# The transfers around a triangular substitution, moved from ScalarE's queue to GpSimd's

## Chip, cores and metric

The kernel runs on one core of a Trainium2 chip. The metric is the time of one execution on the device in microseconds (us). The kernel before was timed in three runs. All times below that have a place in the span are counted from the start of the span of one profiled execution.

## What is computed

One layer of a hybrid encoder on 256 tokens of width 2048: a gated linear attention (GLA) and a gated delta net run side by side on the normalised input, are merged by gates, and are followed by an MLP, a small input embedding and a last norm. The change lies in the delta net. For each head and each chunk of 64 tokens it needs the inverse of a lower triangular matrix:

```python
k_beta = k * beta[..., None]
a = jnp.where(strict, jnp.einsum('bhncd,bhnsd->bhncs', k_beta, k) * decay, 0.0)
t_mat = lax.linalg.triangular_solve(eye + a, jnp.broadcast_to(eye, a.shape), left_side=True,
                                    lower=True, unit_diagonal=True)
u = jnp.einsum('bhncs,bhnsv->bhncv', t_mat, v * beta[..., None])
w = jnp.einsum('bhncs,bhnsd->bhncd', t_mat, k_beta * jnp.exp(gcum)[..., None])
```

## The kernel before

All weights are streamed from HBM in fp32 and multiplied in two parts. The generator `weights` loads 1 MB into `raw` on SyncE's queue, ScalarE rounds it to `whi` (L101), VectorE subtracts to get the rest `wlo` (L102), and TensorE multiplies both parts: L114 to L116 in `stream`, L131 and L135 in `stream_t`. `whi` and `wlo` have three buffers each, so that ScalarE and VectorE may run ahead of TensorE by that much and no more.

The mixers are computed in a loop over four passes (`for h in range(GH)`, L353). A pass makes one GLA head and four delta net heads of two token blocks each, so eight matrices of 128x128. In the order of the program a pass computes k and q of the delta net, the small vectors, and then `af`, the triangular matrices (L459, VectorE). L461 on GpSimd masks their companion `at`.

The inverse is built from diagonal blocks of 32x32. There are 32 of them in a pass, and they are laid out one to a partition so that VectorE can run the substitution on all of them at once:

- `af` goes to DRAM tensor `da` in four DMAs (L468), and comes back as `a32`, 32 partitions of 1024 values (L470). `a32` takes the tile `cacc`, which has one buffer and also serves the short convolution.
- GpSimd has set `t32` to the identity (L472, L473). Then 31 steps of two VectorE instructions each follow, L479 and L481, the first of which waits for `a32`. They lie among the weight splits L102 in VectorE's queue.
- L483 copies the result, transposed within each block, into `u32`, which lies over `a32` in `cacc`. `t32` is stored to `dt` (L484) and `u32` to `du` (L485).
- From there four DMAs fill the diagonal blocks of `u_bd` (L489), two those of `t11` (L491) and one `tb` (L492). Each of them has to wait until `dt` or `du` has landed. TensorE reads them first in L574 to L576, where the off-diagonal blocks are made.

After that the program takes v of the delta net. Its short convolution writes `cacc` anew: four instructions of ScalarE (L378), one per head, and twelve of VectorE (L381), each group after its L378. The first L378 has to wait until `u32` has been read out of `cacc` by the DMA of L485. The weights of the GLA's streams go on at the same time.

All these DMAs are issued by ScalarE (`SC.dma_start`). An engine works through its own queue in order, and a DMA that waits holds up what is queued behind it on the engine that issues it.

Which instruction comes when on each engine isn't written out by hand: the program is given to a planner (`tile.TileContext(nc, schedule_with_timeline_sim=True)`, L864), which plays it through with a model of each instruction and fixes the order on every engine from it. Among instructions that are ready at the same time the one that comes earlier in the program goes first.

Of the kernel before, what the change touches and what calls it, by code (L numbers as in the profile page):

```python
# [37 lines left out]
def hybrid_block(ctx: ExitStack, tc: tile.TileContext, A: dict, out: bass.AP):  # L38
    nc = tc.nc
    V, SC, GP, TE, SY = nc.vector, nc.scalar, nc.gpsimd, nc.tensor, nc.sync  # L40
# [34 lines left out]
    def T4(tag, bufs=None, dt=F32):  # L75
        return mp.tile([P, 4, S], dt, tag=tag, bufs=bufs, name=tag)
# [222 lines left out]
    u_bd = mp.tile([P, 8, P], F32, name="u_bd")  # L299
    t11 = mp.tile([64, 8, 64], F32, name="t11")  # L300
# [52 lines left out]
    for h in range(GH):  # L353
# [58 lines left out]
        for i, src in enumerate((kT, qT)):  # L412
            for t in range(NT):
# [4 lines left out]
                for hd in range(4):  # L418
                    c = i * 8 + t * 4 + hd
# [22 lines left out]
        af = T4("af").rearrange("p a (b c) -> p (a b) c", b=2)  # L442
# [22 lines left out]
        da, dt_, du = (dram.tile([32, 32, 32], F32, name=n) for n in ("da", "dt", "du"))  # L465
        for b in range(4):
            bs = slice(b * 32, (b + 1) * 32)
            SC.dma_start(da[b * 8:(b + 1) * 8].rearrange("i s c -> s i c"), af[bs, :, bs])  # L468
        a32 = T4("cacc")[0:32].rearrange("p a b -> p (a b)").rearrange("p (s c) -> p s c", s=32)
        SC.dma_start(a32, da)  # L470
        t32 = mp.tile([P, NT, 512], F32, tag="og", name="t32").rearrange("p a b -> p (a b)")[0:32]
        GP.memset(t32, 0.0)  # L472
        GP.memset(t32[:, 0:1024:33], 1.0)  # L473
        t32 = t32.rearrange("p (c s) -> p c s", c=32)
# [6 lines left out]
            V.tensor_tensor(t32[:, j + 1:, 0:m], t32[:, j + 1:, 0:m], tv, ALU.subtract)  # L481
        u32 = a32
        V.tensor_copy(u32, t32.rearrange("p c s -> p s c"))  # L483
        SC.dma_start(dt_, t32)  # L484
        SC.dma_start(du, u32)  # L485
        tb = mp.tile([P, 8, 32], F32, tag="tmp", name="tb")
        for b in range(4):
            bs, ds = slice(b * 32, (b + 1) * 32), slice(b * 8, (b + 1) * 8)
            SC.dma_start(u_bd[bs, :, bs], du[ds].rearrange("i s c -> s i c"))  # L489
            if b < 2:  # L490
                SC.dma_start(t11[bs, :, bs], dt_[ds].rearrange("i c s -> c i s"))  # L491
        SC.dma_start(tb[64:96], dt_[16:24].rearrange("i c s -> c i s"))  # L492

        vT = qkv("v", O_DV, 32)
        rv = mp.tile([P, NT, 4, P], F32, name="rv")
# [185 lines left out]
        for kp in range(2):  # L681
            pz = mx3(2, S)
            for kk in range(2):
                for t in range(NT):
                    c = (kp * 2 + kk) * P
# [182 lines left out]
```

## Time and profile before

| | |
|---|---|
| Time, median of 3 runs | 1858.05 us (1855.92 to 1859.32) |
| Time of the profiled execution | 1857.95 us |
| Span of the profiled execution | 1856.2 us |
| TensorE matmuls (PE) busy | 1827.8 us, 98% of the span |
| VectorE (DVE) busy | 1180.2 us, 64% |
| ScalarE (ACT) busy | 946.6 us, 51% |
| GpSimd (POOL) busy | 77.5 us, 4% |
| Mean granted clock of TensorE | 0.996 |
| Bytes moved by DMA | 334.02 MB, 180 GB/s in the mean |

The busy time of an engine doesn't contain the issuing of DMAs on it; those stand in the timeline as ACTq, SPq, or as DMA_DIRECT2D on POOL. The busy time of a matmul is modelled and longer than its step, since matmuls overlap. In the rows a bracket at the end of a line holds the time for which the engine stood before the instruction, and what ended that.

### The profile page before, as it was taken

What the parts mean: (1) busy time and instruction counts of PE and PEld (TensorE: products, weight loads), DVE (VectorE), ACT (ScalarE), POOL (GpSimd) and SP (SyncE); (2) the same over time, 40 slices, a digit from 0 to 9 for tenths busy, and PEclk for the clock granted to TensorE, in tenths of its full rate; (3) what the DMA queues carried; (4) which work ended last, traced back from release to release, by engine and by line L of the source; (5) the groups of instructions that cost most, each with busy time, mean ns of one, the idle gap of its engine ahead of it and who ended that gap; (6) DMA issues with size and microseconds to landing.
All of it is one profiled execution on the core that took longest, in us unless ns stands there. A gap on an engine that the chain in (4) does not pass through costs nothing.

```text
span 1856.2 us, 24598 instructions
## 1 busy us (share of the span) xinstructions
PE 1827.8 (98%) x9796; PEld 1551.0 (84%) x9796; DVE 1180.2 (64%) x1637; ACT 946.6 (51%) x1324; POOL 77.5 (4%) x100
## 2 busy tenths in 40 slices
PE   8999999999999999999999999999999999999998
PEld 7887888878888788887888888888888888888887
DVE  5686577864768647686455655555556555565665
ACT  6745556455564655645545544444444434344654
POOL 3110011000110001100000000000000000000000
PEclk9999999999999999999999999999999999999999
DMA  7555446554455545565465665656656565655453
GB/s 239 148 185 169 159 149 192 168 172 160 155 179 187 178 150 159 159 205 167 144 233 191 184 192 182 198 187 188 196 183 194 191 190 193 187 188 195 162 201 137
DMA packets 245236, 334.02 MB, mean 180 GB/s; under 512 B 21680, under 2 KB 148992, under 8 KB 244736
## 3 DMA queue, kind: packets, MB, share of 16 engines
q1 hardware_dynamic: 231488, 325.47, 54.4%
q10 hardware_dynamic: 12992, 4.34, 1.0%
q0 software_dynamic: 640, 2.63, 0.4%
q8 instruction: 77, 1.26, 0.3%
q14 instruction: 39, 0.32, 0.0%
HBM read 328.74 MB, written 3.67 MB: 179 GB/s over the span
## 4 chain that ended last, share of the span: by engine, by line
PE 92%; DMA 3%; DVE 2%; ACT 2%; issue 1%; ACTq 1%; SPq 0%; POOLq 0%; POOL 0%; DVEq 0%
PE mm L131 24%; PE mm L115 16%; PE mm L116 16%; PE mm L114 16%; PE mm L135 13%; DMA du<-cacc 1%; DMA raw<-in_w_in 1%; PE mx L457 1%; DMA x_sb<-in_x 1%; DVE wlo L102 1%; ACT whi L101 1%; DVE cacc L381 1%; PE mx L562 0%; PE mx L168 0%; ACTq L489 0%
## 5 line engine op out<-in xcount | busy, mean ns | idle before, releaser
L102 DVE TENSOR_TENSOR wlo<-raw,whi 128x1024 fp32r<-128x1024 f32 x604 | 743.8, 1234 | 532.0 <-ACT whi L101 523.3
L101 ACT ACTIVATE whi<-raw 128x1024 fp32r<-128x1024 f32 x604 | 638.8, 1060 | 746.5 <-PE mm L116 389.3
L131 PE MATMUL mm<-act,whi 128*128 128x512 f32 x1984 | 542.7, 395 | 0.0
L131 PEld LDWEIGHTS mm<-act,whi 128*128 128x128 f32 x1984 | 339.7, 189 | 45.8
L115 PE MATMUL mm<-wlo,act 128*128 128x512 f32 x864 | 343.1, 397 | 8.9 <-DVE wlo L102 8.9
L114 PE MATMUL mm<-whi,act 128*128 128x512 f32 x864 | 339.2, 393 | 3.2 <-ACT whi L101 3.2
L135 PEld LDWEIGHTS mm<-act,wlo 128*128 128x128 f32 x1984 | 304.0, 189 | 43.0 <-issue 1.0
L116 PE MATMUL mm<-whi,act 128*128 128x512 f32 x864 | 338.9, 392 | 0.0
L135 PE MATMUL mm<-act,wlo 128*128 128x256 f32 x1984 | 317.4, 281 | 0.0
L115 PEld LDWEIGHTS mm<-wlo,act 128*128 128x128 f32 x864 | 163.1, 189 | 44.0 <-DVE wlo L102 10.4
L116 PE MATMUL mm<-whi,ul 128*128 128x512 f32 x512 | 199.6, 390 | 0.0
L114 PE MATMUL mm<-whi,uh 128*128 128x512 f32 x512 | 199.5, 390 | 0.0
L115 PE MATMUL mm<-wlo,uh 128*128 128x512 f32 x512 | 199.3, 389 | 0.0
L114 PEld LDWEIGHTS mm<-whi,act 128*128 128x128 f32 x864 | 162.8, 188 | 38.3 <-ACT whi L101 4.9
L116 PEld LDWEIGHTS mm<-whi,act 128*128 128x128 f32 x864 | 163.1, 189 | 33.7 <-issue 1.0
L116 PEld LDWEIGHTS mm<-whi,ul 128*128 128x128 f32 x512 | 96.1, 188 | 19.9
L115 PEld LDWEIGHTS mm<-wlo,uh 128*128 128x128 f32 x512 | 96.1, 188 | 19.8
L114 PEld LDWEIGHTS mm<-whi,uh 128*128 128x128 f32 x512 | 96.1, 188 | 19.6
L381 DVE SCALAR_TENSOR_TENSOR cacc<-zT,convw,cacc 128x255 f32<-128x255 f32 (+2 forms) x144 | 61.0, 477 | 18.0 <-ACT cacc L378 18.0
L757 DVE SCALAR_TENSOR_TENSOR x_sb<-mm,r2sq,x_sb 128x512 f32<-128x512 f32 x64 | 45.1, 746 | 12.2 <-PE mm L116 12.2
L479 DVE TENSOR_TENSOR tmp<-cacc,t 32x31 f32<-32x31 f32 (+15 forms) x124 | 40.6, 328 | 4.4 <-DMA cacc<-da 1.5
L481 DVE TENSOR_TENSOR t<-t,tmp 32x31 f32<-32x31 f32 (+15 forms) x124 | 40.8, 329 | 2.8
(311 smaller groups left out, 1230.6 us busy)
## 6 DMA issues: line engine op xcount, KB each, us to landing
raw<-in_w_in SPq DMA_DIRECT2D x143, 1024.0 KB, 4.9
raw<-in_w_up SPq DMA_DIRECT2D x64, 1024.0 KB, 5.6
raw<-in_w_down SPq DMA_DIRECT2D x64, 1024.0 KB, 4.9
raw<-in_w_out SPq DMA_DIRECT2D x16, 1024.0 KB, 4.9
raw<-in_w_ple_gate SPq DMA_DIRECT2D x16, 1024.0 KB, 4.9
x_sb<-in_x POOLq DMA_DIRECT2D x1, 2048.0 KB, 12.4
raw<-in_w_ple_proj SPq DMA_DIRECT2D x4, 512.0 KB, 3.8
out<-x_sb SPq DMA_DIRECT2D x8, 256.0 KB, 2.5
```

The source lines that it names most:

```text
L101: SC.activation(hi[:, :, :c], raw[:, kk:kk + g, :c], AF.Copy)
L102: V.tensor_tensor(lo[:, :, :c], raw[:, kk:kk + g, :c], hi[:, :, :c].bitcast(F32), ALU.subtract)
L114: TE.matmul(pt[:, t, :n], xh[:, k, ts], hi, start=(k == 0), stop=False)
L115: TE.matmul(pt[:, t, :n], xh[:, k, ts], lo, start=False, stop=False)
L116: TE.matmul(pt[:, t, :n], xl[:, k, ts], hi, start=False, stop=(k == nk - 1))
L131: TE.matmul(pt[c // 2][:, c % 2, :], hi[:, c * P:(c + 1) * P], xx[:, k].rearrange("p a s -> p (a s)"), start=(k == 0), stop=False)
L135: TE.matmul(pt[c // 2][:, c % 2, S:2 * S], lo[:, c * P:(c + 1) * P], xh[:, k, :], start=False, stop=(k == nk - 1))
L381: V.scalar_tensor_tensor(acc[:, hd, sh:], zt[:, hd, :S - sh], w(i), acc[:, hd, sh:], ALU.mult, ALU.add)
L457: TE.matmul(pk[:, hd, :], kT[:, hd, ts], rhs[:, hd, ts], start=True, stop=True)
L479: V.tensor_tensor(tv, a32[:, j, j + 1:].unsqueeze(2).to_broadcast([32, n, m]), t32[:, j, 0:m].unsqueeze(1).to_broadcast([32, n, m]), ALU.mult)
L481: V.tensor_tensor(t32[:, j + 1:, 0:m], t32[:, j + 1:, 0:m], tv, ALU.subtract)
L757: V.scalar_tensor_tensor(x_sb[:, t, ns], ps, r2sq[:, t:t + 1], x_sb[:, t, ns], ALU.mult, ALU.add)
```

## The change

The seven `dma_start` lines around the substitution name another queue (some of them stand in a loop, so that they issue 14 DMAs per pass). Sources, targets and sizes stay.

```diff
         for b in range(4):
             bs = slice(b * 32, (b + 1) * 32)
-            SC.dma_start(da[b * 8:(b + 1) * 8].rearrange("i s c -> s i c"), af[bs, :, bs])
+            GP.dma_start(da[b * 8:(b + 1) * 8].rearrange("i s c -> s i c"), af[bs, :, bs])
         a32 = T4("cacc")[0:32].rearrange("p a b -> p (a b)").rearrange("p (s c) -> p s c", s=32)
-        SC.dma_start(a32, da)
+        GP.dma_start(a32, da)
...
-        SC.dma_start(dt_, t32)
-        SC.dma_start(du, u32)
+        GP.dma_start(dt_, t32)
+        GP.dma_start(du, u32)
         tb = mp.tile([P, 8, 32], F32, tag="tmp", name="tb")
         for b in range(4):
             bs, ds = slice(b * 32, (b + 1) * 32), slice(b * 8, (b + 1) * 8)
-            SC.dma_start(u_bd[bs, :, bs], du[ds].rearrange("i s c -> s i c"))
+            GP.dma_start(u_bd[bs, :, bs], du[ds].rearrange("i s c -> s i c"))
             if b < 2:
-                SC.dma_start(t11[bs, :, bs], dt_[ds].rearrange("i c s -> c i s"))
-        SC.dma_start(tb[64:96], dt_[16:24].rearrange("i c s -> c i s"))
+                GP.dma_start(t11[bs, :, bs], dt_[ds].rearrange("i c s -> c i s"))
+        GP.dma_start(tb[64:96], dt_[16:24].rearrange("i c s -> c i s"))
```

## Rows read from the trace of the kernel before

**Rows 1.** Busy us by stretch: length, PE, PEld, DVE, ACT, POOL; PEclk, DMA share, GB/s.

```profile
160.00:170.00 10.00, 7.46 (x32) 5.63 (x30) 5.92 (x12) 5.15 (x8) 0.00 (x0) 0.98 0.59 154
390.00:400.00 10.00, 7.26 (x31) 5.44 (x29) 5.76 (x12) 5.26 (x8) 0.00 (x0) 1.00 0.57 161
620.00:630.00 10.00, 7.39 (x32) 5.58 (x31) 6.40 (x13) 6.91 (x10) 0.00 (x0) 1.00 0.49 129
850.00:860.00 10.00, 6.29 (x25) 4.63 (x24) 6.93 (x14) 7.10 (x10) 0.00 (x0) 0.96 0.38 111
```

**Rows 2.** Timeline of ScalarE, second pass: start us, us, engine, line, operation.

```profile
387.02 0.31 ACTq L485 DMA_DIRECT2D du<-cacc  x1
388.70 1.06 ACT L101 ACTIVATE whi<-raw 128x1024 fp32r<-128x1024 f32 x1 [1.71 <-PE mm L116]
...
391.66 0.84 ACTq L489 DMA_DIRECT2D u_bd<-du  x2
...
394.71 1.71 ACT L378 ACTIVATE cacc<-zT,convw 128x256 f32<-128x256 f32 x4 [4.96 <-issue]
396.33 1.04 ACT L101 ACTIVATE whi<-raw 128x1024 fp32r<-128x1024 f32 x1
```

**Rows 3.** Timeline of TensorE's matmuls, same place.

```profile
396.37 0.39 PE L116 MATMUL mm<-whi,act 128*128 128x512 f32 x1
397.42 0.50 PE L114 MATMUL mm<-whi,act 128*128 128x512 f32 x1 [0.66 <-ACT whi L101]
400.09 0.50 PE L115 MATMUL mm<-wlo,act 128*128 128x512 f32 x1 [2.17 <-DVE wlo L102]
```

**Rows 4.** Timeline of VectorE, second pass, after the substitution.

```profile
395.26 3.65 DVE L381 SCALAR_TENSOR_TENSOR cacc<-zT,convw,cacc 128x255 f32<-128x255 f32 x9 [4.24 <-ACT cacc L378]
398.82 1.22 DVE L102 TENSOR_TENSOR wlo<-raw,whi 128x1024 fp32r<-128x1024 f32 x1
```

**Rows 5.** Busy time by stretch, columns as in group 1: after the first and fourth stall.

```profile
166.50:173.50 7.00, 4.26 (x13) 2.86 (x12) 7.00 (x13) 5.42 (x7) 0.00 (x0) 0.76 0.16 21
853.30:865.00 11.70, 7.99 (x27) 5.90 (x26) 9.23 (x16) 8.34 (x11) 0.00 (x0) 0.85 0.29 92
```

**Rows 6.** Timeline of GpSimd: three places.

```profile
195.14 0.21 POOL L549 MEMSET ga<- 128x128 f32 x1 [85.73 <-PE mx L562]
...
334.79 1.67 POOL L461 TENSOR_TENSOR at<-at,m_incl 128x512 f32<-128x512 f32 x1 [4.96 <-DVE at L459]
...
958.52 0.82 POOL L695 DMA_DIRECT2D x_sb<-in_x  x1 [13.98 <-ACT whi L101]
```

**Rows 7.** Timeline of TensorE, first pass: the first reader of the loaded blocks.

```profile
200.77 0.21 PE L574 MATMUL mx<-t,af 32*32 32x32 f32 x1
```

**Rows 8.** The four stores of du (L485): us from issue to landing.

```profile
DMA to landing us min/median/max: 1.9/4.5/5.2
```

**Rows 9.** DMA issues by tile: engine, operation, count, KB each, median us to landing.

```profile
cacc<-da ACTq DMA_DIRECT2D x4, 128.0 KB, 2.2
...
vec<-in_g_mix ACTq DMA_DIRECT2D x1, 8.0 KB, 3.3
vec<-in_g_mlp POOLq DMA_DIRECT2D x1, 8.0 KB, 5.7
```

**Rows 10.** VectorE's groups by line and form: busy us, mean ns, idle before.

```profile
L102 DVE TENSOR_TENSOR wlo<-raw,whi 128x1024 fp32r<-128x1024 f32 x604 | 743.8, 1234 | 532.0 <-ACT whi L101 523.3 <-PE mm L135 3.5 <-issue 3.2
...
L483 DVE COPY cacc<-t 32x1024 f32<-32x1024 f32 x4 | 4.5, 1137 | 0.1
```

**Rows 11.** Timeline of ScalarE, second pass, before the substitution.

```profile
333.71 1.82 ACTq L468 DMA_DIRECT2D da<-af  x4
335.63 2.01 ACT L101 ACTIVATE whi<-raw 128x1024 fp32r<-128x1024 f32 x2 [5.10 <-DVE zT L362]
...
338.81 1.06 ACT L101 ACTIVATE whi<-raw 128x1024 fp32r<-128x1024 f32 x1 [1.17 <-PE mm L131]
```

**Rows 12.** Timeline of VectorE, second pass, the substitution's start.

```profile
339.13 0.18 DVE L479 TENSOR_TENSOR tmp<-cacc,t 32x31 f32<-32x31 f32 x1
...
340.24 1.20 DVE L102 TENSOR_TENSOR wlo<-raw,whi 128x1024 fp32r<-128x1024 f32 x1
```

## Prediction

> **What bounds the kernel now.** I read the busy time by stretches of 10 us first, because the share over the whole span says only that TensorE is the bound. TensorE is full in nearly every stretch. Four stretches stand out, one for each pass of the head loop: it is busy 7.46, 7.26, 7.39 and 6.29 us of 10 [rows 1]. These are the stretches in which the substitution has just ended and its results go through DRAM on ScalarE's queue, so the timelines of the engines there come next. I take the second pass as the pattern; the other three have the same rows.
>
> ScalarE issues the store of u32 at 387.02, does one weight split (L101) at 388.70, and then stands until dt and du have landed. It issues the two loads of t11 and the four of u_bd, whose first starts at 391.66, and the one of tb. Only at 394.71 does it begin the four L378, and the next weight split comes at 396.33 [rows 2]. TensorE runs out: after the matmul at 396.37 its next two start at 397.42 and 400.09 [rows 3]. One matmul of this stream follows the other by 0.23 us, so the first is 397.42 - 396.37 - 0.23 = 0.82 us late and the second another 400.09 - 397.42 - 0.23 = 2.44 us: 3.26 us in all. The second part is VectorE's: its nine L381 wait for L378, begin at 395.26, and the weight split behind them (L102) begins at 398.82 [rows 4]. In rows 1 this pass shows 2.74 us without work, 0.5 less than the count, because matmuls overlap in the records. With 0.5 added to each pass the stalls are 3.0, 3.3, 3.1 and 4.2 us, 13.6 together. After the first and the fourth the granted clock averaged 0.76 over 7.0 us and 0.85 over 11.7 us [rows 5], between its levels of 2.4 and 1.2 GHz, and TensorE had stood just before: 7.0 x 0.24 + 11.7 x 0.15 = 3.4 us more. So these places hold about **17 us**, and nothing else near the change holds any.
>
> **What moves.** All the DMAs around the substitution leave ScalarE's queue for GpSimd's: five before it (four da, one a32) and nine after (dt, du, four u_bd, two t11, one tb), 14 per pass and 56 in all. No arithmetic changes. GpSimd has room: between L461 and its next instruction, L549 at 195.14, it stands 85.73 us in the first pass [rows 6], and waits of the new DMAs in its queue hold back nothing there. The loads of u_bd, t11 and tb are wanted by TensorE at 200.77 in the first pass [rows 7], over 30 us after ScalarE issued them, so that a few us of delay cost nothing; if this cover were gone, every us of delay would be a us of TensorE.
>
> **After the substitution.** What can't leave is the wait of L378 itself. Its tile has one buffer, the same that du is stored from, so L378 must not begin before du has been read out and landed, whoever issued it. What leaves is the time from that landing to L378. ScalarE's first u_bd load starts when du has landed, at 391.66, L378 at 394.71 [rows 2]: 3.05 us. The same difference in the others is 2.7, 3.1 and 3.4, so 12.3 us in four passes.
>
> Against it stands a longer way for du. No row of before shows this store from GpSimd. From ScalarE it landed after 1.9 to 5.2 us, 4.5 in the median [rows 8]. The nearest rows of GpSimd are the small loads at the start: an 8 KB load took 5.7 us from GpSimd, and one of the same size from ScalarE 3.3 us [rows 9], though at a quieter moment. This gives 0 extra at one end (all of it the traffic beside it) and 5.7 - 3.3 = 2.4 at the other; less than 0 is left out, since every row of GpSimd's loads is longer than ScalarE's of the same size. I take 5.7 - 4.5 = 1.2, since both of these were landed amid other transfers. The delay falls on L378 and on everything behind it: 12.3 - 4 x 1.2 = 7.5 us gained. What is late next is still L102 behind the nine L381, by some 1.4 us of the former 3.26 in this pattern.
>
> The clock's 3.4 us I count as returned, since stalls of 1.2 to 2.0 us are left where 3.0 and 4.2 stood; at the other bound it is 0. The forecast is 7.5 + 3.4 = **10.9 us**; with 0 us extra 15.7, with 2.4 us extra and no clock 2.7.
>
> The Trainium skill (DMA: Bandwidth & Descriptors, Latency and other measured facts) has a first byte after about 1 us from GpSimd and about 0.6 us from SyncE or ScalarE; by it the delay would be an estimated 0.4 us and the gain 14.1.
>
> VectorE's copy L483 runs while GpSimd is to issue dt. It takes 1137 ns for 1024 columns, not much under the 1234 ns of L102, which reads two tensors of 1024 [rows 10], so it runs at the ordinary rate. The Trainium skill (SBUF — State Buffer, SBUF: two separate sides) says that a copy in one of the two-port modes keeps GpSimd from writing descriptors until it ends; by the duration it isn't in one, and were it, dt would be issued at its end and du behind it, an estimated 0.8 us later, which would take 3.3 us off the gain.
>
> **Before the substitution.** In the second pass ScalarE issues the four da in 1.82 us [rows 11]. GpSimd's x_sb, 256 rows of 8 KB, took 0.82 us to issue [rows 6]; a da has 256 rows of 128 B, so four are 3.3 us, 1.5 more. L461 (1.67 us, ready at 334.79) may come between them [rows 6]. Two landings lie in series, da and a32 (2.2 us each before, [rows 9]): 2 x 1.2 = 2.4 us. So a32 arrives 3.9 us later, or 5.5 with L461 between. The first L479 began at 339.13, as a32 landed, with L102 behind it at 340.24 [rows 12]. If VectorE stands so long, TensorE has cover: the L101 at 338.81 had waited for a matmul to give its buffer free [rows 11], so with three buffers TensorE had two groups ahead, each worth 1.71 + 1.06 = 2.8 us by the L101 of rows 2. The third L102 is wanted at 338.81 + 5.6 = 344.4 and would end at 340.24 + 1.2 = 341.4: 3.0 us of cover. So 0.9 to 2.5 us per pass stay uncovered if the order on VectorE is kept, up to 10 us in all. But the order isn't written out: the planner places every instruction on each engine by its own model of transfers, and a later a32 in it puts another L102 ahead of L479, which adds 2.8 us of cover. I take 0, and 10 for the range. ScalarE, which stands before da for 5.1 us [rows 11], gains nothing: TensorE is full there.
>
> **The rivals.**
> - *A weight split gets ahead.* With ScalarE free, the planner may place the next L101 before L378 instead of behind it. Then L102 needn't wait for L378 and the nine L381, and TensorE has 2.8 us more of data than now. For it: ScalarE did take one L101 between du and the loads [rows 2]. Against: L378 stands earlier in the program. All 17 us would go: 1841.
> - *The wait only changes its owner.* du from GpSimd lands 2.4 us later and nearly eats the 3.05 us; the clock falls as before: 2.7 us, 1855. For it: the 5.7 us of the small load, of which 3.3 was reached elsewhere. Against: du itself took up to 5.2 us without GpSimd.
> - *VectorE stands at L479 (slower).* The planner keeps L479 ahead of L102 and L461 goes between the da. At an extra of x us per landing the uncovered wait is 1.5 + 1.67 + 2x - 3.0 per pass, and the gain (15.7 - 4x). They meet at 4 x (0.17 + 2x) = 15.7 - 4x, x = 1.25; above this it is a loss. At x = 2.4 it is 4 x 5.0 = 20 lost against 2.7 gained (no clock returned): 17 slower, 1875. For it: L479 began with no time in hand [rows 12]. Against: it needs the order, L461 and the long landing all together.
>
> **How the numbers follow.** The profiled execution took 1857.95 us (span 1856.2), 0.1 under the median of 1858.05. 1857.95 - 10.9 = **1847**. Chances: forecast 0.45, weight split ahead 0.20, wait only changes owner 0.20, VectorE stands 0.15. Faster by over 0.2% (3.7 us, about what a measurement of this kernel can tell from no change): 0.65; within it 0.20; slower 0.15. The range reaches down to the first rival and up past the second into the milder part of the third, 4 us over the time of before: 1840 to 1862.
>
> **What would show it.** Right: no DMA issue on ScalarE from the da on; L378 begins as du lands, 1 to 2 us earlier relative to the last L101 than now; TensorE's busy time in the four stretches rises from about 7.3 to 8.5 or more of 10, with the clock at 1.00. Wrong: du landing above 7 us; VectorE idle at L479 for more than 3 us with TensorE waiting for L102; or stalls in stretches far from the change, because the planner has ordered something else anew.

## The result and the profile after

The changed kernel took 1846.55 us in the median (1846.42 to 1848.42, four runs), the kernel before 1858.68 on the same chip (1855.92 to 1860.40, four runs). The ratio is 0.9938, 95% interval 0.9921 to 0.9956: faster by 12.1 us, where 10.9 were forecast. The profiled execution took 1846.42 us, its span is 1844.7 us, 11.5 less than before, and the mean granted clock 0.997.

Busy time by stretch, changed kernel, columns as in [rows 1]; the first of the places now lies in the next stretch of 10 us:

```profile
170.00:180.00 10.00, 9.24 (x45) 7.35 (x44) 6.82 (x10) 7.58 (x14) 0.99 (x2) 1.00 0.51 157
390.00:400.00 10.00, 9.11 (x40) 7.00 (x39) 6.89 (x14) 7.93 (x11) 4.07 (x7) 1.00 0.63 214
620.00:630.00 10.00, 8.95 (x39) 6.82 (x38) 8.32 (x15) 8.69 (x12) 3.56 (x7) 1.00 0.45 137
850.00:860.00 10.00, 9.24 (x45) 7.34 (x45) 5.83 (x7) 7.14 (x14) 0.00 (x0) 1.00 0.49 147
```

TensorE now lacks 0.76 + 0.89 + 1.05 + 0.76 = 3.5 us in these four stretches, where it lacked 11.6 in [rows 1], and the granted clock is 1.00 in all four and in the stretches behind them, where it was 0.76 and 0.85 for a while [rows 5]. So 8.1 us came from the stalls and, by the estimate made for [rows 5], 3.4 from the clock: 11.5, which is the difference of the two spans.

ScalarE in the second pass, then VectorE and TensorE at the same place (compare [rows 2], [rows 4] and [rows 3]):

```profile
390.13 1.06 ACT L101 ACTIVATE whi<-raw 128x1024 fp32r<-128x1024 f32 x1 [1.66 <-PE mm L116]
393.10 1.71 ACT L378 ACTIVATE cacc<-zT,convw 128x256 f32<-128x256 f32 x4 [1.91 <-DMA du<-cacc]
394.83 1.28 ACT L655 ACT_TABLE_LOAD   x1
396.12 1.27 ACT L655 ACTIVATE gate<-mm,r 128x512 f32<-128x512 f32 x2
397.28 2.00 ACT L101 ACTIVATE whi<-raw 128x1024 fp32r<-128x1024 f32 x2
...
393.64 4.04 DVE L381 SCALAR_TENSOR_TENSOR cacc<-zT,convw,cacc 128x255 f32<-128x255 f32 x10 [1.20 <-ACT cacc L378]
398.37 1.23 DVE L102 TENSOR_TENSOR wlo<-raw,whi 128x1024 fp32r<-128x1024 f32 x1 [0.69 <-ACT whi L101]
...
397.86 0.39 PE L116 MATMUL mm<-whi,act 128*128 128x512 f32 x1
398.39 0.50 PE L114 MATMUL mm<-whi,act 128*128 128x512 f32 x1
399.65 0.50 PE L115 MATMUL mm<-wlo,act 128*128 128x512 f32 x1 [0.76 <-DVE wlo L102]
```

No DMA stands between du's landing and L378 any more: the row of L378 names du's landing as what ended its wait. From the last L101 before L378 to L378 it is 393.10 - 390.13 = 2.97 us; before it was 394.71 - 388.70 = 6.01 [rows 2]. The 3.0 us between are the 3.05 of the prediction. But a stall is left: 398.39 - 397.86 - 0.23 = 0.30 and 399.65 - 398.39 - 0.23 = 1.03, together 1.33 us in this pass where it was 3.26 [rows 3]. And it has a new cause. Between L378 and the next L101 now stand a table load and the two gates of the gg stream (L655), 2.55 us; in the kernel before, two L101 came first. VectorE's L102 waits 0.69 us for its L101. The gates themselves have not moved: counted in weight splits they stand at the same place. Up to the gates of the second pass (398.33 before, 394.83 after) ScalarE has done the same number of L101, first before, then after:

```profile
L101 ACT ACTIVATE whi<-raw 128x1024 fp32r<-128x1024 f32 x122 | 128.7, 1059 | 127.7 <-PE mm L116 52.7 <-PE mm L131 49.6 <-issue 5.9
...
L101 ACT ACTIVATE whi<-raw 128x1024 fp32r<-128x1024 f32 x122 | 128.8, 1060 | 134.5 <-PE mm L116 63.2 <-PE mm L131 49.0 <-issue 7.6
```

It is L378 that has moved: by the same count it stood behind 120 of them and now stands behind 122, directly ahead of the gates.

The landings of the DMAs in question, after (us in the last column; before: du 4.5 by [rows 8], cacc 2.2 by [rows 9]):

```profile
cacc<-da POOLq DMA_DIRECT2D x4, 128.0 KB, 3.9
du<-cacc POOLq DMA_DIRECT2D x4, 128.0 KB, 4.4
```

In the median the store of du takes no longer from GpSimd than from ScalarE (in the first pass it took 3.8 us where ScalarE's took 1.9, in the other three 4.2 to 4.6 against 4.3 to 5.2). The load of a32 does take longer, by 1.7 us.

The start of the substitution, second pass, GpSimd and VectorE (compare [rows 11] and [rows 12]):

```profile
330.00 2.40 POOL L468 DMA_DIRECT2D da<-af  x4 [3.01 <-DVE af L459]
332.41 1.31 POOL L461 TENSOR_TENSOR at<-at,m_incl 128x512 f32<-128x512 f32 x1
335.11 0.54 POOL L470 DMA_DIRECT2D cacc<-da  x1 [1.39 <-DVE wlo L102]
...
338.72 1.23 DVE L102 TENSOR_TENSOR wlo<-raw,whi 128x1024 fp32r<-128x1024 f32 x1 [1.57 <-ACT whi L101]
339.86 0.17 DVE L479 TENSOR_TENSOR tmp<-cacc,t 32x31 f32<-32x31 f32 x1
```

The planner put all four da ahead of L461, and two more L102 ahead of the first L479 than in the kernel before, in each of the four passes; VectorE stands at L479 only in the first pass (0.7 us, where the kernel before had 1.5), and TensorE is full there.

### The profile page after: what moved, and what is told of

It reads as the page before. It is cut to its first block, busy times and chain, and to the rows that moved or that the text cites. A ratio compares the mean times of both kernels' runs of the same rounds, so it can differ in the third digit from the quotient of the medians.

```text
span 1844.7 us, 24633 instructions
## 1 busy us (share of the span) xinstructions
PE 1823.3 (99%) x9796; PEld 1547.4 (84%) x9796; DVE 1183.0 (64%) x1637; ACT 947.5 (51%) x1324; POOL 111.7 (6%) x156
## 4 chain that ended last, share of the span: by engine, by line
PE 82%; issue 12%; DMA 2%; ACT 2%; DVE 1%; POOL 0%; SPq 0%; POOLq 0%; ACTq 0%; DVEq 0%
PE mm L131 23%; PE mm L115 14%; PE mm L116 13%; PE mm L114 13%; PE mm L135 11%; DMA du<-cacc 1%; DMA x_sb<-in_x 1%; DMA raw<-in_w_in 1%; PE mx L457 1%; ACT whi L101 1%; PE mx L562 0%; PE mx L168 0%; DVE wlo L102 0%; ACT cacc L378 0%; PE mx L532 0%
## 5 line engine op out<-in xcount | busy, mean ns | idle before, releaser
L102 DVE TENSOR_TENSOR wlo<-raw,whi 128x1024 fp32r<-128x1024 f32 x604 | 745.0, 1236 | 520.4 <-ACT whi L101 513.0
L101 ACT ACTIVATE whi<-raw 128x1024 fp32r<-128x1024 f32 x604 | 638.0, 1060 | 762.0 <-PE mm L116 413.4
L115 PE MATMUL mm<-wlo,act 128*128 128x512 f32 x864 | 340.8, 394 | 3.3 <-DVE wlo L102 3.3
L135 PEld LDWEIGHTS mm<-act,wlo 128*128 128x128 f32 x1984 | 304.4, 189 | 43.4 <-issue 1.0
L114 PE MATMUL mm<-whi,act 128*128 128x512 f32 x864 | 339.3, 393 | 0.4 <-ACT whi L101 0.3
L116 PE MATMUL mm<-whi,act 128*128 128x512 f32 x864 | 337.3, 390 | 0.0
L135 PE MATMUL mm<-act,wlo 128*128 128x256 f32 x1984 | 317.9, 281 | 0.0
L116 PE MATMUL mm<-whi,ul 128*128 128x512 f32 x512 | 199.6, 390 | 0.0
L114 PE MATMUL mm<-whi,uh 128*128 128x512 f32 x512 | 199.5, 390 | 0.0
L115 PE MATMUL mm<-wlo,uh 128*128 128x512 f32 x512 | 199.3, 389 | 0.0
L115 PEld LDWEIGHTS mm<-wlo,act 128*128 128x128 f32 x864 | 162.3, 188 | 38.3 <-DVE wlo L102 4.8
L114 PEld LDWEIGHTS mm<-whi,act 128*128 128x128 f32 x864 | 162.3, 188 | 35.0 <-ACT whi L101 1.9
L116 PEld LDWEIGHTS mm<-whi,act 128*128 128x128 f32 x864 | 162.3, 188 | 33.6 <-issue 1.0
L116 PEld LDWEIGHTS mm<-whi,ul 128*128 128x128 f32 x512 | 96.1, 188 | 20.0
L114 PEld LDWEIGHTS mm<-whi,uh 128*128 128x128 f32 x512 | 96.1, 188 | 19.8
L115 PEld LDWEIGHTS mm<-wlo,uh 128*128 128x128 f32 x512 | 96.1, 188 | 19.6
L381 DVE SCALAR_TENSOR_TENSOR cacc<-zT,convw,cacc 128x255 f32<-128x255 f32 (+2 forms) x144 | 60.3, 478 | 5.1 <-ACT cacc L378 5.1
```

The costliest lines, as they stand in the source:

```text
L101: SC.activation(hi[:, :, :c], raw[:, kk:kk + g, :c], AF.Copy)
L102: V.tensor_tensor(lo[:, :, :c], raw[:, kk:kk + g, :c], hi[:, :, :c].bitcast(F32), ALU.subtract)
L114: TE.matmul(pt[:, t, :n], xh[:, k, ts], hi, start=(k == 0), stop=False)
L115: TE.matmul(pt[:, t, :n], xh[:, k, ts], lo, start=False, stop=False)
L116: TE.matmul(pt[:, t, :n], xl[:, k, ts], hi, start=False, stop=(k == nk - 1))
L135: TE.matmul(pt[c // 2][:, c % 2, S:2 * S], lo[:, c * P:(c + 1) * P], xh[:, k, :], start=False, stop=(k == nk - 1))
```

## The experiments

In every run the kernel before ran on the same chip beside it; ratios are to it, with 95% intervals. "Nine" are the transfers behind the substitution (dt, du, four u_bd, two t11, one tb), "five" those ahead of it (four da, a32).

**Which of the transfers pay.** Four kernels each move a part of the fourteen to GpSimd.

```diff
 nine only  (e1): L484, L485, L489, L491, L492   SC -> GP
 five only  (e2): L468, L470                     SC -> GP
 seven loads(e3): L489, L491, L492               SC -> GP
 two stores (e4): L484, L485                     SC -> GP
```

> Only the nine transfers behind the substitution (dt, du, four u_bd, two t11, one tb) go to GpSimd; the four da and a32 stay on ScalarE. All of the reference is computed. Theory: what paid is that ScalarE no longer waits and issues for the nine. In the kernel after, du landed 4.4 us after its issue on GpSimd (median) against 4.5 us on ScalarE before, so nothing is lost in the landing, and L378 should start within about 0.3 us of du's landing. The stall then falls by the 2.7 to 3.4 us per pass that lay between du's landing and L378, 12.3 us in all, and the clock gives 3.4 us back: about 1842 to 1845 us, no more than the 1846.5 of the whole change. Rival: what paid is that moving da and a32 made the planner put more weight splits (L101, L102) ahead; then this kernel has less than half of the gain, 1852 us or more.

Measured: 1844.76 us against 1860.32, ratio 0.9916 (0.9901 to 0.9930), as the theory had it.

> Only the seven loads behind the substitution (u_bd, t11, tb) go to GpSimd; the two stores dt and du, and the five transfers ahead of it, stay on ScalarE. All of the reference is computed. Theory: the stores cost ScalarE only their issue (0.3 to 0.5 us each), and what costs is the loads, which wait in ScalarE's queue for the stores to land, ahead of L378 and L101: nearly all of the gain, 1842 to 1848 us. Rival: the stores too must leave, since they stand in ScalarE's queue behind VectorE's L483 and hold the L101 behind them: half of the gain at most, 1852 us or more.

Measured: 1843.97 us, ratio 0.9911 (0.9897 to 0.9926). The theory held.

> The counterpart of the one before: only the two stores dt and du go to GpSimd; the seven loads stay on ScalarE. All of the reference is computed. Theory: no gain, 1855 to 1860 us: ScalarE still stands at the first load of t11 or u_bd until a store has landed, with L378 behind all seven. Rival: the stores were what blocked, 1850 us or less.

Measured: 1859.03 us, ratio 0.9990 (0.9979 to 1.0001): no gain clear of the noise, as expected.

> Only the four da and a32, ahead of the substitution, go to GpSimd; the nine behind it stay on ScalarE. All of the reference is computed. Theory: these five are worth nothing, as TensorE is full there: 1856 to 1860 us, with the same four stalls of about 3 us each and the clock below 1.00 after at least one of them. Rival: the planner's order, moved by these five, is what paid: about 1850 us, with an L101 more ahead of L378 than before. A third possibility: VectorE stands at L479 for the later a32: 1862 us or more.

Measured: 1870.51 us, ratio 1.0054 (1.0039 to 1.0069): 10 us slower, which was the third possibility by its size, but not by its mechanism, as shown below.

The seven loads carry the whole gain. ScalarE in the second pass, first with only the two stores moved, then with only the seven loads moved:

```profile
388.66 0.31 ACTq L491 DMA_DIRECT2D t<-dt  x1
389.01 0.97 ACTq L489 DMA_DIRECT2D u_bd<-du  x2
...
391.67 0.41 ACTq L492 DMA_DIRECT2D tb<-dt  x1
392.12 1.71 ACT L378 ACTIVATE cacc<-zT,convw 128x256 f32<-128x256 f32 x4 [5.00 <-issue]
```

```profile
383.49 0.31 ACTq L485 DMA_DIRECT2D du<-cacc  x1
385.17 1.06 ACT L101 ACTIVATE whi<-raw 128x1024 fp32r<-128x1024 f32 x1 [1.72 <-PE mm L116]
387.92 1.71 ACT L378 ACTIVATE cacc<-zT,convw 128x256 f32<-128x256 f32 x4 [1.69 <-DMA du<-cacc]
389.54 2.07 ACT L101 ACTIVATE whi<-raw 128x1024 fp32r<-128x1024 f32 x2
```

With the loads on ScalarE, L378 starts 392.12 - 389.01 = 3.1 us after the first u_bd load could start, and these us are filled with issues of 0.3 to 0.6 us. So the 3 us were not a wait of ScalarE for anything: they were its own work of issuing seven DMAs, at the one moment when L378 had become ready. With the loads elsewhere, L378 starts 387.92 - 383.49 = 4.4 us after du's issue, which is du's landing, and two L101 follow at once.

**Why the five cost time.** TensorE's waits by releaser (total us, times, longest), five only:

```profile
PE mm L114 <- ACT whi L101: 12.3, 4, 3.6
PE mm L135 <- DVE wlo L102: 3.3, 3, 1.1
PE mm L115 <- DVE wlo L102: 3.3, 6, 0.8
```

and its ScalarE in the second pass:

```profile
398.00 1.06 ACT L101 ACTIVATE whi<-raw 128x1024 fp32r<-128x1024 f32 x1 [0.41 <-PE mm L116]
...
405.26 1.28 ACT L655 ACT_TABLE_LOAD   x1
406.55 1.26 ACT L655 ACTIVATE gate<-mm,r 128x512 f32<-128x512 f32 x2
407.71 2.95 ACT L101 ACTIVATE whi<-raw 128x1024 fp32r<-128x1024 f32 x3
```

VectorE doesn't stand at L479 in this kernel either (0.7 us in the first pass, nothing in the others); the loss lies at the far end, where L378 is again late by the seven issues and, on top of it, the table load and gates come before the L101: 407.71 - 398.00 = 9.7 us without a weight split, where the kernel before had 396.33 - 388.70 = 7.6 [rows 2]. In the kernel after and in this one, which move the five, L655 has this place in all four passes; in the kernel before and in those with the nine, the loads or the stores alone, one or two L101 come ahead of it. Again it isn't the gates that move: in all of these kernels, and in every pass, they stand behind the same L101. With the five on GpSimd a32 comes later, two more L102 go ahead of the first L479, the substitution ends one or two weight splits later, and L378 comes two later, which puts it directly ahead of the gates. Two kernels pin the gates behind the fourth L101 of the next stream, one made from the changed kernel, one from the kernel with the five alone:

```diff
-        stream([... O_GG ...], KD, hT, ev_silu("gg"))
-        stream([... O_GA ...], KD, hT, ev_sig("gg", gnw))
+        stream([... O_GG ...], KD, hT, lambda t, ps: held.append((ev_silu("gg"), t, ps)))
+        stream([... O_GA ...], KD, hT, ev_sig("gg", gnw), held)
 # in stream:
-        for pair in weights(srcs, nk):
+        for i, pair in enumerate(weights(srcs, nk)):
+            if i == 3:
+                with tc.issue_after(weights.last.ins):
+                    [f(t, ps) for f, t, ps in held]
```

> The changed kernel itself once more, as the yardstick for the three beside it: a ratio to the kernel before of 0.992 to 0.996, with 1.3 us of stall per pass behind L378 (an L115 that waits for VectorE's L102).

Measured: 1847.08 us (1845.80 to 1847.60) against 1861.21, ratio 0.9927 (0.9914 to 0.9940).

> The changed kernel with one order pinned: the two gates of the gg stream (L655, with their table load of 1.28 us and 1.27 us of work) are put behind the fourth weight split (L101) of the next stream, so that two L101 stand between L378 and them, as they do in the kernel before. All of the reference is computed. Theory: what the changed kernel has left of its stalls, 1.3 us per pass, comes from those 2.55 us on ScalarE ahead of the L101 that TensorE wants next. VectorE's L102 began 0.69 us late for that L101 and one L381 later than it could, so 0.8 to 1.1 us per pass come back, 3 to 4 us, and the time equals that of the kernel with only the nine moved (a ratio to before of about 0.991 to 0.992). Rival: the nine L381 ahead of L102 set the time and the gates are hidden: less than 1 us.

Measured: 1844.42 us (1844.06 to 1844.71), ratio 0.9914 (0.9900 to 0.9928): 2.7 us less than the changed kernel beside it, a little under the expected 3 to 4, and the level of the nine alone.

> The kernel with only the five transfers ahead of the substitution on GpSimd (1870.5 us), and in it the same pinned order as before: the gates L655 behind the fourth L101 of the next stream. All of the reference is computed. Theory: moving the five costs time only through the order that the planner makes of it, above all the gates ahead of the L101s behind L378; with them behind, the stall there falls from 3.8 us per pass to the 3.0 of the kernel before, and less of the clock is lost: 1858 to 1864 us. Rival: the later end of the substitution (8 us later than in the kernel before) costs by itself: 1867 us or more.

Measured: 1856.16 us (1853.46 to 1858.27), ratio 0.9980 (0.9970 to 0.9990). One pinned order took 14 us from the kernel with the five, more than expected. ScalarE and TensorE's waits in it (the inserted lines shift the numbers: L116 and L117 here are L114 and L115 of the other kernels):

```profile
400.28 1.71 ACT L378 ACTIVATE cacc<-zT,convw 128x256 f32<-128x256 f32 x4 [4.41 <-issue]
401.90 1.99 ACT L101 ACTIVATE whi<-raw 128x1024 fp32r<-128x1024 f32 x2
403.90 1.28 ACT L655 ACT_TABLE_LOAD   x1
```

```profile
PE mm L117 <- DVE wlo L102: 8.6, 4, 2.2
PE mm L116 <- ACT whi L101: 2.0, 4, 0.8
```

The substitution still ends later in it (L485 at 392.89 where it was 387.02 in [rows 2], and two weight splits later) and the seven loads are still on ScalarE, so neither of these alone is what made the five dear: that the gates follow directly on L378 is. The waits on L101 fell from 12.3 to 2.0 us and those on L102 rose from 3.3 to 8.6, so that what is left looks like the kernel before. A part of the 14 us comes from other places, since the pin moves later instructions too: the L135 waits of 3.3 us, for instance, are down to 0.6. How much each place owes to the gates themselves wasn't separated. Why the planner keeps the gates at their place while L378 moves isn't shown; its own times aren't in a trace.

**The shared tile.** Here u32 gets the place of `rv`, which is free at that time, so that L378 no longer waits for du at all: once in the kernel before (ScalarE issues everything), once in the changed kernel, once with the nine alone moved.

```diff
-        u32 = a32
+        u32 = mp.tile([P, NT, 4, P], F32, name="rv")[0:32].rearrange(...)
```

> The kernel before (all transfers on ScalarE's queue), and only u32 is given the place of rv, so that L378 needn't wait for du. All of the reference is computed. Theory: the wait of the loads in ScalarE's queue holds every L101 behind them whether L378 waits for the tile or not; half of the loss or less goes, 1850 us or more (ratio 0.995 or more). Rival: the shared tile alone was the cause, and the queue is harmless once L378 is done ahead of the loads: 1842 to 1845 us (ratio 0.991 to 0.992).

Measured: 1844.46 us (1843.84 to 1846.19), ratio 0.9916 (0.9901 to 0.9931). The theory fell, the rival held.

> The changed kernel, and u32 is given the place of rv (free there) in place of a32's, so that L378 no longer waits for du to land. All of the reference is computed. Theory: the shared tile's wait is the last part of the stall; L378 and the nine L381 come 3 to 4 us earlier, and no stall of TensorE is left there: 5 us less than the changed kernel, a ratio to before of about 0.991. Rival: the planner spends the room on other work and some 1 us per pass stays: 0.993 to 0.994.

Measured: 1843.90 us (1843.06 to 1844.54), ratio 0.9913 (0.9896 to 0.9929): the theory's ratio, and no stall of TensorE is left there, but 3.2 us less than the changed kernel beside it, not 5. Of this the tile's own part isn't separate: without the wait for du L378 stands again where it stood in the kernel before, with L101 between it and the gates, and that alone was worth 2.7 us above.

> Both cures together: the nine transfers behind the substitution on GpSimd, the five ahead of it on ScalarE, and u32 in the place of rv so that L378 needn't wait for du. All of the reference is computed. Theory: both remove the same path (du's landing, L378, the nine L381, L102), so they don't add: 1842.5 to 1845 us, the same as with either. Rival: each has removed a part of its own, and together they give more: 1841 us or less.

Measured: 1842.34 us (1841.43 to 1842.59) against 1860.02, ratio 0.9901 (0.9884 to 0.9918): the lowest of all, though its interval overlaps with that of either cure alone, so whether the two add anything stays open. It fell between the theory's 1842.5 and the rival's 1841.

The first of the three is the one to look at. All transfers are on ScalarE's queue, as before. ScalarE, VectorE and TensorE in the second pass:

```profile
383.91 1.06 ACT L101 ACTIVATE whi<-raw 128x1024 fp32r<-128x1024 f32 x1 [0.39 <-PE mm L116]
386.64 0.32 ACTq L491 DMA_DIRECT2D t<-dt  x1
...
389.50 0.47 ACTq L492 DMA_DIRECT2D tb<-dt  x1
390.06 1.28 ACT L384 ACT_TABLE_LOAD   x1 [5.09 <-DVE cacc L381]
...
392.32 1.99 ACT L101 ACTIVATE whi<-raw 128x1024 fp32r<-128x1024 f32 x2
...
382.12 3.23 DVE L381 SCALAR_TENSOR_TENSOR cacc<-zT,convw,cacc 128x255 f32<-128x255 f32 x8
393.39 2.36 DVE L102 TENSOR_TENSOR wlo<-raw,whi 128x1024 fp32r<-128x1024 f32 x2 [4.20 <-ACT whi L101]
...
392.47 1.09 PE L499 MATMUL mx<-ident,Tv 128*128 128x128 f32 x8 [0.42 <-ACT Tv L384]
394.67 0.50 PE L115 MATMUL mm<-wlo,act 128*128 128x512 f32 x1 [0.19 <-DVE wlo L102]
```

ScalarE stands and issues as long as ever: from one L101 to the next it is 392.32 - 383.91 = 8.4 us, more than the 7.6 of the kernel before. Yet TensorE loses 0.42 + 0.19 = 0.6 us by the rows (nothing in the first pass, 1.0 and 1.1 us in the last two). The difference is VectorE: the L381 were done early, at 382.12, and the L102 follows its L101 at once, while in the kernel before it waited for nine L381 behind a late L378 [rows 4]. So ScalarE's long absence is nearly covered by the buffers of `whi` and `wlo`; what cost most was the chain du's landing, L378, L381, L102.

**Another queue.** The nine on SyncE's queue, which feeds all weight loads.

```diff
 L484, L485, L489, L491, L492:  SC.dma_start -> SY.dma_start
```

> The nine transfers behind the substitution go to SyncE's queue, which issues the weight loads (raw, 1 MB each, landed after 4.9 us in the median); the five ahead of it stay on ScalarE. All of the reference is computed. Theory: a waiting transfer is dear only on a queue with other work behind it, and SyncE has some: a raw load that stands behind dt, du and the seven loads is held for about 8 us (du's 4.5 us of landing and seven issues of about 0.5 us). A raw load is wanted every 5.4 us (two L101 of 2.72 us) and there are three buffers, so one has 10.9 - 4.9 = 6.0 us in hand: 2 us of stall per pass, 1848 to 1855 us. Rival: the raw loads have enough in hand, and any queue but ScalarE's does as well as GpSimd's: 1843 to 1846 us.

Measured: 1843.08 us (1842.66 to 1843.53), ratio 0.9906 (0.9891 to 0.9920). The rival held. SyncE's queue in the second pass:

```profile
376.40 5.81 SPq L93 DMA_DIRECT2D raw<-in_w_in  x2
382.30 0.45 SPq L484 DMA_DIRECT2D dt<-t  x1
...
390.31 0.45 SPq L492 DMA_DIRECT2D tb<-dt  x1
390.81 16.45 SPq L93 DMA_DIRECT2D raw<-in_w_in  x4
```

It was kept from raw loads for 390.81 - 382.2 = 8.6 us, as expected, but the theory had counted all of this as delay. The load behind could not have gone before its buffer came free: the L102 that reads it last ended at 387.26, 5.4 us after the load ahead was issued. So it was late by 390.81 - 387.26 = 3.55 us, and it had 6.0 in hand.

## Why the prediction was right, point by point

The time was forecast to 0.5 us (1847.0 against 1846.55), but not because every term was: two missed by several us each and cancelled, the longer landing of du (4.8 us taken, about 0 measured) and the stage ahead of the substitution (0 taken, about 3 lost). That the sum came out so close is luck; the bound and what leaves it were right.

- **The bound and its size, right.** The four stalls and the clock held 17 us; the kernel with both cures gained 1860.02 - 1842.34 = 17.7. The 3.4 us of the clock in it are an estimate.
- **The 3.05 us between du's landing and L378, right in size.** It is gone in the changed kernel and alone carries the gain, as the seven loads show. That the loads' readers have cover held as well: L574 has its blocks, and TensorE doesn't stand there [rows 7]. The text let a "wait" leave; it was seven issues, one after the other.
- **The longer landing of du, wrong.** Taken as 1.2 us, it is about 0: 4.4 us from GpSimd against 4.5 from ScalarE in the median. The bound of 0 was in the sum, and with it the gain was 15.7; the nine alone, where the stage ahead is left as it was, gained 1860.32 - 1844.76 = 15.6. The two small loads at the start from which the 2.4 came [rows 9] are no measure for a store in the middle of the stream. The first-byte figures of the Trainium skill (DMA: Bandwidth & Descriptors, Latency and other measured facts) would have put an estimated 0.4 us there; no run shows it in du, whose landing was 4.2 us from GpSimd in the kernels with the nine and with the two stores alone.
- **The stage ahead of the substitution at 0, wrong in its place.** What was looked for there was right: L461 could have come between (it came behind), four da took 2.40 us (3.3 were estimated), a32 landed after 3.9 us instead of 2.2 (3.4 estimated), the planner put more L102 ahead of L479 (two, not one), and nothing was lost at that place. But those two splits were paid for at the other end: the substitution ended later by one or two of them, L378 by two, and so it fell directly ahead of the gates. By the pinned order this costs 2.7 us in the changed kernel, and 14 (a part of it at other places) where the loads are still on ScalarE. The step that failed is the sentence that takes 0 because the planner "puts another L102 ahead": an order that is made anew was followed only to the first place where it helps.
- **What is late next, right in size by luck and wrong in name.** About 1.4 us of stall per pass were left as forecast (1.33 in the second). But the forecast's 1.4 held the 1.2 us of du's longer landing, which wasn't there, and laid them on the nine L381. With the nine alone L102 begins directly behind them and no stall of this size is left (0.7 us over the four passes together); what was late in the changed kernel was the L101 behind the gates.
- **The clock, right.** 1.00 at and behind all four places, with stalls of 1.0 to 1.5 us left. After the 4 us stall of the kernel with the five alone it falls again: 0.77 and 0.89 in the two stretches of 10 us from 170 us on, and 0.83 in one stretch at each of its other three stalls.
- **The rivals.** "A weight split gets ahead" did not occur in its form in the last three passes (one L101 stands between du's issue and L378, as before; in the first there is now one where there was none), but its time of 1841 is near where the kernel with both cures ends. "The wait only changes its owner" needed du to land 2.4 us later and fell. "VectorE stands at L479" was sized at 17 us of loss; a loss of 10 us did show with the five alone, at another place and by another mechanism. VectorE did stand there once, in the kernel with both cures: 4.4 us in the fourth pass, where a32 landed after 4.9 us. TensorE lost 0.35 us in the 6 us behind it, so the cover there was larger than the 3.0 us counted.

## What to carry to other kernels

A DMA cost the engine that issued it 0.3 to 0.7 us here, with few exceptions, and seven in a row cost most where they stand directly ahead of an instruction that has just become ready and that others wait for; such issues belong on a queue where nothing is due, and here SyncE's and GpSimd's did equally. Before moving a queue, ask what the waiting instruction waits for: here one tile shared by two users made the wait, and giving the second its own place won the same without moving anything. Where a planner orders the program, a change that has no cost where it stands may still be paid further on, where what it delays meets other work, so compare the order behind the change's far end too, counted in instructions that both kernels have; moving the parts one by one shows it, since they don't add (15.6 us gained, 10.2 lost, together 12 to 14 gained).

## What the runs showed of the hardware that was not expected

GpSimd's issue of dt ends with VectorE's copy. VectorE and GpSimd, changed kernel, second pass:

```profile
387.13 1.12 DVE L483 COPY cacc<-t 32x1024 f32<-32x1024 f32 x1
...
387.65 0.71 POOL L484 DMA_DIRECT2D dt<-t  x1 [52.00 <-issue]
388.55 0.49 POOL L485 DMA_DIRECT2D du<-cacc  x1 [0.19 <-issue]
```

The copy ends at 388.25 and the issue at 388.36. In the first pass the issue starts 0.27 us earlier against the copy and takes 0.98 us instead of 0.71, and again ends 0.10 us behind it; so it is in all four passes of the changed kernel, of the one with the nine and of the one with the two stores (0.09 to 0.11 us, twelve of twelve). ScalarE's issue of dt beside the same copy, in the kernel before, took 0.32 us and ended 0.7 to 0.8 us ahead of the copy's end. The prediction had taken from the copy's duration that it doesn't hold GpSimd up. It does. The Trainium skill (SBUF — State Buffer, SBUF: two separate sides) says that an fp32 copy from SBUF to SBUF triggers a two-port mode, during which GpSimd can't write descriptors, and the rows agree with that. Only the price was small: du has to wait for the copy anyway and is issued 0.30 us after its end (from ScalarE it was 0.03 us), not the 0.8 us later that were estimated.

A load of 128 KB from DRAM (a32) landed after 3.9 us from GpSimd and after 2.2 from ScalarE [rows 9], the store of the same size (du) after 4.4 and 4.5. Why the load is slower and the store isn't wasn't tried. It isn't so of every load: those of t11 (32 KB) landed 1.9 to 2.2 us after their issue from GpSimd in the last three passes of the kernel with both cures, and 1.6 to 2.2 from SyncE.
